# The order of large and small experts in a routed layer, small experts two chunks behind

## The chip, the cores and the metric

The kernel runs on one core of one Trainium2 chip. The metric is the device time of one execution in microseconds (us); each kernel is run several times and the median counts. All operands and results are float32; weights arrive from HBM in units of [128 x 2048] float32, 1 MB (1.0486 million bytes) each. Matrix products of the large experts are made of three products of rounded parts (float32r), those of the small experts of plain float32 ones.

## The reference, cut to what matters

Two decoder layers on 256 tokens of width 1024. Layer 0: differential attention beside a state-space model, then a dense SwiGLU. Layer 1: two kinds of attention, then eight routed SwiGLU experts of which each token uses two. The change touches the experts alone:

```python
def swiglu(h, w_gate, w_up, w_down):
    return (jax.nn.silu(h @ w_gate) * (h @ w_up)) @ w_down

def moe_swiglu(h, router, w_gate, w_up, w_down):
    ...
    logits = (t @ router).astype(jnp.float32)
    top_val, top_idx = lax.top_k(logits, TOP_K)
    top_w = jax.nn.softmax(top_val, axis=-1)
    gates = jnp.sum(jax.nn.one_hot(top_idx, N_EXPERTS, dtype=jnp.float32) * top_w[..., None], axis=1)
    for e in range(N_EXPERTS):
        out = out + gates[:, e:e + 1].astype(t.dtype) * swiglu(t, w_gate[e], w_up[e], w_down[e])
```

D_MODEL is 1024, D_FF 2816, N_EXPERTS 8, TOP_K 2.

## The kernel before, in words

The experts are put in order of their number of tokens at run time. The four with the most are called large (up to 128 tokens, kept in a tile of 128), the four with the fewest small (up to 64, kept in a tile of 64). If an expert has more than 128 tokens, a loop behind an `If` takes the rest; it does not run here. D_FF is cut in 11 chunks of 256. A chunk of an expert has three units of weights: two halves of the gate and up weights (`gu` unit 0 and 1, each 512 of the 1024 input rows) and one unit of the down weights (`dn`). Four large and four small experts make 88 chunks and 264 units.

A **large** chunk: each unit is split into a rounded part `wh` (ScalarE, `ACTIVATE wh`) and the rest `wl` (VectorE, `TENSOR_TENSOR wl`) by `split`, and each half of the gate and up product (`ff_gu`, 12 matmuls, L517 to L519, stationary `fh`, `fl`) and the down product (`ff_dn`, 12 matmuls, stationary `tw`) use them. Between them stand Silu and the multiplication (`ff_act`) and two transpositions on TensorE with their copies (`ff_tr`). A **small** chunk uses the weights as they arrive, in products on half of the array's columns (128*64, two at a time): `sm_gu` (8 matmuls of 256 columns a half unit pair, shown as 16 by the profile), `sm_act`, one transposition in `sm_tr`, `sm_dn` (4 matmuls of 512 columns, shown as 8). The products of an expert's chunks add up in two PSUM tiles; after its last chunk they are split (`y_split`) and scattered to the tokens (`scatter`, 8 matmuls). The tokens of an expert are gathered ahead by one-hot matmuls (`gather_all`, two or four of them a group).

`Stream` (L693) reads the units in the order of use. It has nine places that a unit can land in (five `raw`, and `xres`, `xg`, `more`, `fl`; a tenth until unit 14), and four pairs of tiles for `wh` and `wl` (`HL` = 4). A large unit's place comes free when it is split, a small unit's when TensorE has used it; SP issues the next unit's load into the place that came free first, and waits for it in order. `st.ahead(n)` splits the next large unit if fewer than n are split and unused.

Up to the first expert the order on each engine is written by a recording scheduler (`Recorder`); in the experts' stage the recorder is off (`rec.on = False`) and each engine does its instructions in the order in which the Python code writes them. That order is what the change edits. Before: `items` holds the chunks, large ones alone for the first four (`LAG` = 4), then large and small in turn, then four small ones. In the step of item i stand: first half of its gate and up product, the transpositions of item i-1 and its copies, a split ahead, the second half, Silu, the down product of item i-1. A small item's halves therefore have the transpositions of a large chunk between them, and a large item's halves that of a small chunk. The gathers and the scatter stand behind the down product.

Of the kernel before, what the change touches and what calls it, by code (L numbers as in the profile page):

```python
# [19 lines left out]
P = 128  # L20
EPS = 1e-6
NEG = -1e30
FC = 11
# [26 lines left out]
HL = 4  # L50
# [2 lines left out]
XG = 14  # L53
BIG = 4
HALFP = 64
LAG = 4
PAIRED = 0.65
WARM = 10
FIRST = 9
# [335 lines left out]
def kernel(ctx: ExitStack, tc: tile.TileContext, a, out: bass.AP):  # L395
# [32 lines left out]
    def pa():  # L428
        return rec.tile(psp, [P, 512], F32, "ps", 8, name="ps")
# [337 lines left out]
    def ff_gu(st, xs, gu, u, ahead=True):  # L767
        wh, wl = st.next(ahead)
        for b in range(len(xs)):
            for kk in range(4):  # L770
                k = 4 * u + kk
                mm3(gu[b], xs[b][0][:, k, :], xs[b][1][:, k, :], wh[:, kk * 512:(kk + 1) * 512],
                    wl[:, kk * 512:(kk + 1) * 512], k == 0, k == 7)

    def ff_act(gu, scales=None, act=None):
        hs = []
        for b in range(len(gu)):
            si = tw(256)
            hh = tw(256)
            if scales:  # L780
                tact(si, gu[b][:, 0:256], AF.Silu, scale=scales[b])
                V.scalar_tensor_tensor(hh, gu[b][:, 256:512], scales[b], si, op0=OP.mult, op1=OP.mult)
            else:
                (act or tact)(si, gu[b][:, 0:256], AF.Silu)
                V.tensor_tensor(hh, gu[b][:, 256:512], si, OP.mult)
            hs.append(hh)
        return hs

    def ff_tr(hs):
        n = 2 * len(hs) * P  # L790
        tp = pa()
        transposes([h[:, i * P:(i + 1) * P] for i in range(2) for h in hs], tp)
        th, tl = tw(n, dt=F32R), tw(n, dt=F32R)
        S.activation(th, tp[:, :n], AF.Copy)
        V.tensor_tensor(tl, tp[:, :n], th.bitcast(F32), OP.subtract)
        return th, tl

    def ff_dn(st, t, yps, first, last, ahead=True):
        wh, wl = st.next(ahead)
        nb = len(yps)  # L800
        order = [(b, i, hf) for b in range(nb) for i in range(2) for hf in range(2)]
        for b, i, hf in sorted(order, key=lambda o: o[2]) if last else order:
            rec.late = HALF if last and hf else 0
            sl = slice((i * nb + b) * P, (i * nb + b + 1) * P)
            ws = slice(i * 1024 + hf * 512, i * 1024 + (hf + 1) * 512)
            mm3(yps[b][hf], t[0][:, sl], t[1][:, sl], wh[:, ws], wl[:, ws], first and i == 0, last and i == 1)
# [63 lines left out]
    for g in range(2):  # L870
        ps = [pa() for i in range(2)]
        for u in range(2):
            wh, wl = split(raw0[u]) if g == 0 else unit(a["w0"][2 + u])
            for kk in range(4):
                k = 4 * u + kk
# [8 lines left out]
        for c in range(4):  # L884
            j = 4 * g + c
# [93 lines left out]
    for b in range(2):  # L979
        y = tw()  # L980
# [529 lines left out]
    def y_split(yps):  # L1510
        rec.late = 0
        y = [(tw(dt=F32R), tw(dt=F32R)) for i in range(2)]
        for i in range(2):
            rec.late = HALF if i else 0
            S.activation(y[i][0], yps[i], AF.Copy)
            V.tensor_tensor(y[i][1], yps[i], y[i][0].bitcast(F32), OP.subtract)
        return y

    def scatter(t, y, g, acc, store=False):
        for i in range(2):  # L1520
            rec.late = HALF if i else 0
            cs = slice(i * 512, (i + 1) * 512)
            for b in range(2):
                sp = pa()
                T.matmul(sp, t[:, b * P:(b + 1) * P], y[i][0], start=True, stop=False)
                T.matmul(sp, t[:, b * P:(b + 1) * P], y[i][1], start=False, stop=True)
                V.scalar_tensor_tensor(acc[:, b, cs], sp, g(b), acc[:, b, cs], op0=OP.mult, op1=OP.add)
                if store:
                    dma(ov[:, b, cs], acc[:, b, cs])
        rec.late = 0  # L1530
# [5 lines left out]
    def large_split(src):  # L1536
        x = large_tile()
        S.activation(x[0], src, AF.Copy)
        V.tensor_tensor(x[1], src, x[0].bitcast(F32), OP.subtract)
        return x  # L1540


    def sm_gu(xs, gu, u):
        w = st.next(False)
        for kk in range(4):
            k = 4 * u + kk
            wv = w[:, kk * 512:(kk + 1) * 512].rearrange("p (g f) -> p g f", g=2)
            for i in range(2):
                mmx(gu[i * HALFP:(i + 1) * HALFP, 0:256].rearrange("p (g f) -> p g f", g=2), xs[:, k],
                    wv[:, :, i * P:(i + 1) * P], k == 0, k == 7)  # L1550
        st.done()

    def sm_act(gu):
        si, hh = tw(P), tw(P)
        tact(si, gu[:, 0:P], AF.Silu)
        V.tensor_tensor(hh, gu[:, P:256], si, OP.mult)
        return hh

    def sm_tr(hh):
        tp = pa()  # L1560
        transposes([hh], tp)
        t = tw(P)
        S.activation(t, tp[:, 0:P], AF.Copy)
        return t
# [14 lines left out]
        return lambda: gtile([P, 2048], F32, n, 2) if n == "xres" else mo([P, 2048], n)  # L1579


    items = []
    for g in range(BIG * FC + LAG):
        if g < BIG * FC:
            items.append((False, *divmod(g, FC)))
        if g >= LAG:
            items.append((True, *divmod(g - LAG, FC)))
    regs = {}

    def source(r, j):  # L1590

        if r == 0:
            return a["moe"][j]

        def at_run():
            if r not in regs:
                regs[r] = nc.values_load(ids[0:1, r:r + 1], engines=[mybir.EngineType.SP], min_val=0, max_val=7)
            return a["moe"][bass.ds(regs[r] * (3 * FC) + j, 1)].rearrange("u p c -> p (u c)")
        return at_run

    srcs, whole = [], []
    for i in range(len(items) + 1):
        for it, js in ((items[i] if i < len(items) else None, (0, 1)), (items[i - 1] if i else None, (2,))):
            for j in js if it else ():
                srcs.append(source(it[1] + (BIG if it[0] else 0), 3 * it[2] + j))
                whole.append(it[0])
    st = Stream(srcs, ([(place("xres"), 999), (place("xg0"), XG)],
                       [(place("xg1"), 999), (place("more"), 999), (place("fl"), 999)]), whole)
    xb = large_tile()
# [6 lines left out]
    xs = top([P, BIG, 8, HALFP], "xs")  # L1616
    oh_s = one_hots(BIG, BIG, HALFP)
    ov = out.rearrange("(b p) d -> p b d", p=P)
    ys, ohs, ohts, hs, pend = {}, {}, {}, {}, None
    N = len(items)  # L1620
    for i in range(N + 1):
        it = items[i] if i < N else None
        was = items[i - 1] if i else None
        alone = not (it and was and it[0] != was[0])
        if it:
            sm, p, c = it
            gu = pa()
            xsp = xs[:, p] if sm else [xb]
            sm_gu(xsp, gu, 0) if sm else ff_gu(st, xsp, [gu], 0, False)
        if was:  # L1630
            t = sm_tr(hs[was]) if was[0] else ff_tr(hs[was])
        st.ahead(HL if alone or it[0] else HL - 1)
        if it:
            sm_gu(xsp, gu, 1) if sm else ff_gu(st, xsp, [gu], 1, False)
            hs[it] = sm_act(gu) if sm else ff_act([gu])
            if not sm and c == FC - 1 and p < BIG - 1:
                xb = large_split(xl[:, p % 2])
        if alone or it[0]:
            st.ahead(HL)
        if was:  # L1640
            wsm, wp, wc = was
            if wc == 0:
                ys[wsm] = [pa(), pa()]
            (sm_dn if wsm else lambda t, y, *f: ff_dn(st, t, [y], *f, False))(t, ys[wsm], wc == 0, wc == FC - 1)
            if alone:
                st.ahead(HL)
        if pend:
            scatter(*pend)
            pend = None
        if was and was[2] == FC - 1:  # L1650
            r = was[1] + (BIG if was[0] else 0)
            pend = (ohts[was[0]], y_split(ys[was[0]]), lambda b, r=r: gateo[:, b, r:r + 1], x3, i == N)
        if not it:
            continue
        if c == 0:
            ohs[sm] = both_halves(BIG + p) if sm else one_hots(p, 1)[:, :, 0]
        if c == 1:
            ohts[sm] = oht_of(ohs[sm][:, 0], ohs[sm][:, 1])
        if sm:
            continue  # L1660
        if p == 0 and c < LAG:
            for k in range(2 * c, 2 * c + 2):
                gather_all(k, oh_s, xs)
        if p == 0 and LAG + 2 <= c < LAG + 6:
            if c == LAG + 2:
                xl, oh_l = mo([P, 2, 8, P], "xg0"), one_hots(1, 2)
            for k in range(2 * (c - LAG - 2), 2 * (c - LAG - 1)):
                gather_all(k, oh_l, xl)
        if p == 1 and 2 <= c < 6:
            if c == 2:  # L1670
                oh_l = one_hots(3, 1)
            for k in range(2 * c - 4, 2 * c - 2):
                gather_all(k, oh_l, xl[:, 0:1])
    scatter(*pend)
    man.close()


# [177 lines left out]
```

## Time and profile before

| what | value |
|---|---|
| time, median of 3 runs | 1151.35 us (1151.13 to 1151.51) |
| the profiled execution's own time | 1150.8 us |
| its span | 1148.9 us, mean granted clock 0.994 |
| TensorE (PE) busy | 1124.3 us, 98% |
| VectorE (DVE) busy | 714.2 us, 62% |
| ScalarE (ACT) busy | 587.3 us, 51% |
| HBM read, written | 345.95 MB, 1.05 MB |
| experts' stage, from the first large product to the last down product | 468 to 1139 us |

A busy time of TensorE is a union of overlapping matmuls whose ends are modelled; how long a piece of its work takes is read from the start of one piece to the start of the next. Times of rows count from the start of the span. In the rows of a timeline, `x16` is a run of 16 instructions of one kind, and `[0.62 <-DVE tw L333]` is idle time ahead of it and what ended it. L333 is a helper's line, which stands for many operations; the tiles tell them apart: `ps<-cp,tw` is a transposition, `ps<-tw,xnh` and `ps<-tw,xnl` a gather, `ps<-tw` a scatter, 128*64 a small expert's product.

### The profile page before, as it was taken

To read this page: it belongs to the slowest core of one execution; us is meant where nothing else is said; L and a number is where in the kernel's file an instruction comes from. 1 tells how busy PE (TensorE), PEld (TensorE's weight loads), DVE (VectorE), ACT (ScalarE), POOL (GpSimd) and SP (SyncE) were. 2 spreads that over 40 slices of the span, in tenths; PEclk is the share of its full clock that TensorE was granted. 3 is DMA by queue.
4 is the path that set the end of the run, shared out by engine and by line. 5 is a ranking of instruction groups with operands and counts; after the bars stand their busy time and mean duration, and the time that the engine had idled before them with its cause. 6 is when DMAs were issued, how large, how long until landed. Compare 5 with 4: busy or idle time off the path is not lost.

```text
span 1148.9 us, 16368 instructions
## 1 busy us (share of the span) xinstructions
PE 1124.3 (98%) x6100; PEld 825.4 (72%) x6100; DVE 714.2 (62%) x1172; ACT 587.3 (51%) x979; POOL 29.6 (3%) x59
## 2 busy tenths in 40 slices
PE   8999999999999999999999999999999999999997
PEld 7887888888787877876666666666666666666663
DVE  6999954545388877784456456556556556565531
ACT  6858644444378666573545444444444444444421
POOL 1050000000300000000000000000000000000000
PEclk9999999999999999899999999999999999999999
DMA  9651555546344514389999999999999999999994
GB/s 353 224 198 37 195 208 189 189 179 219 112 167 154 216 63 188 117 325 373 374 404 419 399 400 392 393 424 422 421 421 422 422 423 420 422 421 418 421 421 157
DMA packets 52214, 348.14 MB, mean 303 GB/s; under 512 B 5920, under 2 KB 6048, under 8 KB 11680
## 3 DMA queue, kind: packets, MB, share of 16 engines
q1 hardware_dynamic: 52128, 347.02, 76.1%
q8 instruction: 50, 0.82, 0.3%
q14 instruction: 36, 0.29, 0.1%
HBM read 345.95 MB, written 1.05 MB: 302 GB/s over the span
## 4 chain that ended last, share of the span: by engine, by line
PE 84%; DMA 7%; DVE 5%; ACT 3%; issue 1%; SPq 0%; DVEq 0%; ACTq 0%
PE ps L333 21%; PE ps L517 18%; PE ps L519 18%; PE ps L518 18%; PE ps L328 10%; DMA xres<-in_moe_dram 7%; DVE wl L333 2%; ACT wh L333 2%; DVE wl L328 1%; ACT tw L328 1%; DVE xres L333 0%; DVE tw L328 0%; DMA raw<-in_w_dram 0%; DVE tw L333 0%; DVE more L328 0%
## 5 line engine op out<-in xcount | busy, mean ns | idle before, releaser
L333 DVE TENSOR_TENSOR wl<-raw,wh 128x2048 fp32r<-128x2048 f32 x89 | 204.2, 2294 | 149.5 <-ACT wh L333 148.0
L517 PE MATMUL ps<-wh,fh 128*128 128x512 f32 (+2 forms) x720 | 290.9, 404 | 0.0
L518 PE MATMUL ps<-wl,fh 128*128 128x512 f32 (+2 forms) x720 | 280.6, 390 | 0.0
L333 ACT ACTIVATE tw<-ps 128x128 f32<-128x128 f32 (+2 forms) x202 | 72.7, 362 | 312.1 <-PE ps L333 275.6
L333 ACT ACTIVATE wh<-raw 128x2048 fp32r<-128x2048 f32 x89 | 170.0, 1910 | 62.3 <-PE ps L519 57.7
L517 PEld LDWEIGHTS ps<-wh,fh 128*128 128x128 f32 x720 | 136.4, 189 | 28.1
L518 PEld LDWEIGHTS ps<-wl,fh 128*128 128x128 f32 x720 | 136.4, 189 | 24.1
L333 DVE TENSOR_TENSOR tw<-ps,tw 128x256 f32<-128x256 f32 (+3 forms) x158 | 66.7, 427 | 135.6 <-ACT tw L333 135.5
L519 PE MATMUL ps<-wh,fl 128*128 128x512 f32 (+2 forms) x368 | 142.1, 386 | 0.0
L519 PE MATMUL ps<-wh,fh 128*128 128x512 f32 x352 | 139.0, 395 | 0.0
L333 DVE TENSOR_TENSOR wl<-xres,wh 128x2048 fp32r<-128x2048 f32 x39 | 89.3, 2289 | 53.5 <-ACT wh L333 53.5
L333 PE MATMUL ps<-raw,xs 128*64 128x256 f32 x960 | 116.3, 384 | 0.0
L517 PE MATMUL ps<-wh,tw 128*128 128x512 f32 (+1 forms) x276 | 113.9, 413 | 0.7 <-ACT tw L328 0.7
L519 PE MATMUL ps<-wh,tw 128*128 128x512 f32 (+1 forms) x276 | 109.0, 395 | 0.0
L518 PE MATMUL ps<-wl,tw 128*128 128x512 f32 (+1 forms) x276 | 108.8, 394 | 0.0
L333 ACT ACTIVATE wh<-xres 128x2048 fp32r<-128x2048 f32 x39 | 74.8, 1917 | 63.4 <-DMA xres<-in_moe_dram 58.6
L328 DVE TENSOR_TENSOR wl<-raw,wh 128x512 fp32r<-128x512 f32 (+1 forms) x149 | 98.3, 683 | 2.7 <-ACT wh L328 2.7
L333 PEld LDWEIGHTS ps<-raw,xs 128*64 128x64 f32 x960 | 64.8, 137 | 41.3 <-issue 14.5
L328 ACT ACTIVATE wh<-raw 128x512 fp32r<-128x512 f32 (+1 forms) x131 | 74.8, 626 | 20.1 <-PE ps L519 8.6
L519 PEld LDWEIGHTS ps<-wh,fl 128*128 128x128 f32 x368 | 69.1, 188 | 14.3 <-DVE fl L328 0.2
L519 PEld LDWEIGHTS ps<-wh,fh 128*128 128x128 f32 x352 | 66.7, 189 | 14.5
L517 PEld LDWEIGHTS ps<-wh,tw 128*128 128x128 f32 x276 | 52.0, 188 | 26.4 <-issue 15.4
(283 smaller groups left out, 1324.9 us busy)
## 6 DMA issues: line engine op xcount, KB each, us to landing
raw<-in_moe_dram SPq DMA_DIRECT2D x142, 1024.0 KB, 9.6
xres<-in_moe_dram SPq DMA_DIRECT2D x41, 1024.0 KB, 10.5
raw<-in_ffn_dram SPq DMA_DIRECT2D x30, 1024.0 KB, 4.8
xg<-in_moe_dram SPq DMA_DIRECT2D x27, 1024.0 KB, 9.8
more<-in_moe_dram SPq DMA_DIRECT2D x26, 1024.0 KB, 10.8
fl<-in_moe_dram SPq DMA_DIRECT2D x25, 1024.0 KB, 9.7
raw<-in_w_dram SPq DMA_DIRECT2D x23, 1024.0 KB, 5.0
raw<-in_ffn_dram SPq DMA_DIRECT2D x12, 256.0 KB, 3.7
```

Of the source, the lines that this page charges most:

```text
L328: return (self.name, self.cost(fn, args, kw), lambda: real(*args, **kw))
L333: return getattr(self.eng, fn)(*args, **kw)
L517: nc.tensor.matmul(ps, xh, wh, start=start, stop=False)
L518: nc.tensor.matmul(ps, xh, wl, start=False, stop=False)
L519: nc.tensor.matmul(ps, xl, wh, start=False, stop=stop)
```

## The change

`LAG` goes from 4 to 2. The list of items becomes a list of steps (`tr` transpositions, `gu0` and `gu1` the halves, `dn` down product, `late` scatter, `rest` gathers and one-hots, `more` a split ahead), written once for each chunk of the large experts. In the mixed stretch it is: transpositions of the last large chunk, first half of the next, the scatter if there is one, the small chunk's transposition, large down product, second half, gathers, and then the three small units in one block: down product, first half, second half. A split ahead (now always to four) stands behind each transposition and behind the large down product. The eight gathers of the small experts come four a chunk in the first two large chunks instead of two a chunk in the first four.

```diff
-LAG = 4
+LAG = 2
...
-    items = []
-    for g in range(BIG * FC + LAG):
-        if g < BIG * FC:
-            items.append((False, *divmod(g, FC)))
-        if g >= LAG:
-            items.append((True, *divmod(g - LAG, FC)))
+    steps = []
+    for g in range(BIG * FC + LAG + 1):
+        l, l0, s, s0 = chunk(False, g), chunk(False, g - 1), chunk(True, g - LAG), chunk(True, g - LAG - 1)
+        if l and s0:
+            o = [("tr", l0), ("gu0", l), ("late", None), ("tr", s0), ("dn", l0), ("gu1", l), ("rest", l),
+                 ("dn", s0), ("gu0", s), ("gu1", s)]
+        elif l0:
+            o = [("gu0", l), ("tr", l0), ("gu0", s if not l else None), ("tr", s0), ("gu1", l), ("more", l), ("dn", l0),
+                 ("late" if l else "", None), ("rest", l), ("dn", s0), ("gu0", s if l else None), ("gu1", s)]
+        else:
+            o = [("gu0", l or s), ("tr", s0), ("gu1", l or s), ("more", l), ("dn", s0), ("late", None), ("rest", l)]
+        steps += [(k, it) for k, it in o if it or k == "late"]
...
-        st.ahead(HL if alone or it[0] else HL - 1)
...
+        elif k == "tr":
+            ts[sm] = sm_tr(hs[sm]) if sm else ff_tr(hs[sm])
+            st.ahead(HL)
+        elif k == "dn":
...
+                ff_dn(st, ts[sm], [ys[sm]], c == 0, c == FC - 1, False)
                 st.ahead(HL)
...
-            for k in range(2 * c, 2 * c + 2):
-                gather_all(k, oh_s, xs)
...
+                for j in range(8 // LAG * c, 8 // LAG * (c + 1)):
+                    gather_all(j, oh_s, xs)
```

On TensorE, in the mixed stretch, the small block and what follows it. `raw`, `more` and `xres` are places of small units, `cp` is the identity for a transposition. Before:

```order
L519 MATMUL ps<-wh,fh 128x512
L333 MATMUL ps<-raw,tw 64x512 x4
L333 MATMUL ps<-more,xs 64x256 x8
L333 MATMUL ps<-cp,tw 128x128 x2
L333 MATMUL ps<-raw,xs 64x256 x8
L517 MATMUL ps<-wh,tw 128x512
```

And the changed kernel at a like place:

```order
L519 MATMUL ps<-wh,fh 128x512
L333 MATMUL ps<-raw,tw 64x512 x4
L333 MATMUL ps<-raw,xs 64x256 x8
L333 MATMUL ps<-xres,xs 64x256 x8
L333 MATMUL ps<-cp,tw 128x128 x2
L517 MATMUL ps<-wh,fh 128x512
```

The large chunk's two transpositions moved from between the small halves to behind them, and behind them comes the large first half (stationary `fh`) where the large down product (stationary `tw`) came.

On ScalarE, one pair of a large and a small chunk. `wh` is a split, `tw` of 128x256 the large chunk's Silu or the copy behind its transpositions, `tw` of 128x128 the same of the small chunk. Before:

```order
L333 ACTIVATE wh<-raw 128x2048
L333 ACTIVATE tw<-ps 128x256 x2
L333 ACTIVATE wh<-fl 128x2048
L333 ACTIVATE tw<-ps 128x128
L333 ACTIVATE wh<-xres 128x2048
L333 ACTIVATE tw<-ps 128x128
```

And the changed kernel:

```order
L333 ACTIVATE tw<-ps 128x256
L333 ACTIVATE wh<-raw 128x2048
L333 ACTIVATE tw<-ps 128x128
L333 ACTIVATE wh<-more 128x2048
L333 ACTIVATE wh<-fl 128x2048
L333 ACTIVATE tw<-ps 128x256
L333 ACTIVATE tw<-ps 128x128
```

The three splits of a pair, which stood apart with one or two other instructions between them, stand closer: two of them follow each other, with the large chunk's Silu (128x256) right behind.

## Rows read from the trace of the kernel before

**Rows 1.** Two stretches: busy of PE, PEld, DVE, ACT, POOL; PEclk; DMA share; GB/s.
```profile
505.00:767.00 262.00, 260.88 (x1434) 175.53 (x1433) 144.25 (x129) 123.84 (x142) 0.00 (x0) 1.00 0.98 394
767.00:1110.00 343.00, 342.36 (x1861) 228.78 (x1860) 198.16 (x176) 157.44 (x169) 0.00 (x0) 1.00 1.01 421
```
**Rows 2.** Timeline of TensorE over one pair: start, us, instruction, run.
```profile
745.35 0.39 PE L519 MATMUL ps<-wh,fh 128*128 128x512 f32 x1
745.67 1.94 PE L333 MATMUL ps<-raw,tw 128*64 128x512 f32 x8
747.44 1.90 PE L333 MATMUL ps<-xg,xs 128*64 128x256 f32 x16
749.27 0.44 PE L333 MATMUL ps<-cp,tw 128*128 128x128 f32 x2
749.63 1.95 PE L333 MATMUL ps<-raw,xs 128*64 128x256 f32 x16
751.51 0.50 PE L517 MATMUL ps<-wh,tw 128*128 128x512 f32 x1
...
754.42 0.39 PE L517 MATMUL ps<-wh,fh 128*128 128x512 f32 x1
...
757.16 0.27 PE L333 MATMUL ps<-cp,tw 128*128 128x128 f32 x1
757.18 0.48 PE L517 MATMUL ps<-wh,fh 128*128 128x512 f32 x1
...
760.11 1.94 PE L333 MATMUL ps<-more,tw 128*64 128x512 f32 x8
```
**Rows 3.** Waits from 520 to 1110 us: who for whom, total us, times, longest.
```profile
ACT wh L333 <- DMA xres<-in_moe_dram: 58.6, 23, 4.3
...
PE ps L333 <- DVE tw L333: 1.8, 3, 0.6
```
**Rows 4.** The chain of waits, 937 to 953 us: start, us, what.
```profile
937.76 10.51 DMA xres<-in_moe_dram
...
948.34 1.93 ACT wh L333
...
952.61 11.61 DMA xres<-in_moe_dram
```
**Rows 5.** Timeline of TensorE where small chunks run alone.
```profile
1126.84 1.95 PE L333 MATMUL ps<-more,xs 128*64 128x256 f32 x16
1128.61 1.89 PE L333 MATMUL ps<-raw,tw 128*64 128x512 f32 x8
```
**Rows 6.** Timeline of TensorE where large chunks run alone.
```profile
479.75 0.38 PE L333 MATMUL ps<-cp,tw 128*128 128x128 f32 x2
479.88 0.48 PE L517 MATMUL ps<-wh,fh 128*128 128x512 f32 x1
...
482.71 0.40 PE L517 MATMUL ps<-wh,tw 128*128 128x512 f32 x1
```
**Rows 7.** The chain of waits at two pairs with a gather.
```profile
574.17 7.14 PE ps L333 x50
589.90 7.13 PE ps L333 x50
```
**Rows 8.** Timeline of TensorE at a gather with a wait, and at a scatter.
```profile
544.37 0.63 PE L333 MATMUL ps<-tw,xnh 128*128 128x256 f32 x2 [0.62 <-DVE tw L333]
...
790.86 2.11 PE L333 MATMUL ps<-tw 128*128 128x512 f32 x8
792.90 1.95 PE L333 MATMUL ps<-raw,xs 128*64 128x256 f32 x16
```
**Rows 9.** DMA from 505 us to the end: queue total; issues, KB, median us to landing.
```profile
q1 hardware_dynamic: 36853, 255.78, 96.9%
...
xg<-in_moe_dram SPq DMA_DIRECT2D x4, 256.0 KB, 5.3
```
**Rows 10.** Timeline of SP at the last loads: the last unit's four quarters.
```profile
1124.26 2.16 SPq L443 DMA_DIRECT2D xg<-in_moe_dram  x4
```

More of the change, by code (lines that the diff above doesn't have):

```diff
@@ L1579, in place, with chunk @@
         return lambda: gtile([P, 2048], F32, n, 2) if n == "xres" else mo([P, 2048], n)
-    items = []
-    for g in range(BIG * FC + LAG):
-        if g < BIG * FC:
-            items.append((False, *divmod(g, FC)))
-        if g >= LAG:
-            items.append((True, *divmod(g - LAG, FC)))
+    def chunk(sm, g):
+        return (sm, *divmod(g, FC)) if 0 <= g < BIG * FC else None
+    steps = []
[10 more added lines that the diff above has]
+        steps += [(k, it) for k, it in o if it or k == "late"]
     regs = {}
@@ L1599, in source @@
         return at_run
[L1601 to L1606, printed above, removed]
+    unit_of = {"gu0": 0, "gu1": 1, "dn": 2}
+    used = [(k, it) for k, it in steps if k in unit_of]
+    srcs = [source(it[1] + (BIG if it[0] else 0), 3 * it[2] + unit_of[k]) for k, it in used]
+    whole = [it[0] for k, it in used]
     st = Stream(srcs, ([(place("xres"), 999), (place("xg0"), XG)],
@@ L1618 @@
     ov = out.rearrange("(b p) d -> p b d", p=P)
[L1619 to L1631, printed above, removed]
-        st.ahead(HL if alone or it[0] else HL - 1)
[L1633 to L1638, printed above, removed]
-            st.ahead(HL)
[L1640 to L1645, printed above, removed]
-                st.ahead(HL)
[L1647 to L1661, printed above, removed]
-            for k in range(2 * c, 2 * c + 2):
-                gather_all(k, oh_s, xs)
[L1664 to L1673, printed above, removed]
@@ L1674 @@
-    scatter(*pend)
+    gu, hs, ts, ys, ohs, ohts, pend = {}, {}, {}, {}, {}, {}, []
+    for n, (k, it) in enumerate(steps):
+        if k == "late":
+            while pend:
+                scatter(*pend.pop(0))
+            continue
+        sm, p, c = it
+        if k == "more":
+            st.ahead(HL)
+        elif k in ("gu0", "gu1"):
+            if k == "gu0":
+                gu[sm] = pa()
+            if sm:
+                sm_gu(xs[:, p], gu[sm], unit_of[k])
+            else:
+                ff_gu(st, [xb], [gu[sm]], unit_of[k], False)
+            if k == "gu1":
+                hs[sm] = sm_act(gu[sm]) if sm else ff_act([gu[sm]])
+                if not sm and c == FC - 1 and p < BIG - 1:
+                    xb = large_split(xl[:, p % 2])
+                if c == 0:
+                    ohs[sm] = n, both_halves(BIG + p) if sm else one_hots(p, 1)[:, :, 0]
+        elif k == "tr":
+            ts[sm] = sm_tr(hs[sm]) if sm else ff_tr(hs[sm])
+            st.ahead(HL)
+        elif k == "dn":
+            if c == 0:
+                ys[sm] = [pa(), pa()]
+            if sm:
+                sm_dn(ts[sm], ys[sm], c == 0, c == FC - 1)
+            else:
+                ff_dn(st, ts[sm], [ys[sm]], c == 0, c == FC - 1, False)
+                st.ahead(HL)
+            if c == FC - 1:
+                r = p + (BIG if sm else 0)
+                pend.append((ohts[sm], y_split(ys[sm]), lambda b, r=r: gateo[:, b, r:r + 1], x3, n == len(steps) - 2))
+        else:
+            for e in list(ohs):
+                if n >= ohs[e][0] + 5:
+                    o = ohs.pop(e)[1]
+                    ohts[e] = oht_of(o[:, 0], o[:, 1])
+            if p == 0 and c < LAG:
+                for j in range(8 // LAG * c, 8 // LAG * (c + 1)):
+                    gather_all(j, oh_s, xs)
+            if p == 0 and LAG + 2 <= c < LAG + 6:
+                if c == LAG + 2:
+                    xl, oh_l = mo([P, 2, 8, P], "xg0"), one_hots(1, 2)
+                for j in range(2 * (c - LAG - 2), 2 * (c - LAG - 1)):
+                    gather_all(j, oh_l, xl)
+            if p == 1 and 2 <= c < 6:
+                if c == 2:
+                    oh_l = one_hots(3, 1)
+                for j in range(2 * c - 4, 2 * c - 2):
+                    gather_all(j, oh_l, xl[:, 0:1])
```

## The prediction

> **What bounds the kernel now.** I read the stretches of the expert stage first, to see which engine is full. TensorE is busy throughout, at a granted clock of 1.00, and the DMA engines have a share of 0.98 at 394 GB/s from 505 to 767 us and of 1.01 at 421 GB/s from 767 to 1110 us [rows 1]. Both look full, and a busy share does not tell who waits for whom. So I went to TensorE's instructions in order of time. One pair (the three units of a large chunk and the three of a small one) runs from 745.67 to 760.11 us, 14.44 us, without an idle time worth naming [rows 2]; from 520 to 1110 us the largest wait of TensorE for another engine sums to 1.8 us [rows 3]. TensorE sets the pace. But the weights are close behind: one pair needs six units of 1.0486 MB, which at 421 GB/s take 14.94 us, more than the pair's 14.44. That the memory stream has caught up shows in the chain of waits: a landing in `xres`, on its way from 937.76 us, releases ScalarE's split at 948.34, which with VectorE's releases the next landing at 952.61 [rows 4], a loop of 14.85 us; and ScalarE waited 58.6 us in 23 places for such landings, 4.3 us at most [rows 3]. TensorE hardly felt these, because the weights are split well ahead of their use. So there are two limits half a microsecond a pair apart, and the change moves only one of them.
>
> **The change part by part.** No product is added or removed: 36 large and 20 small products and three transpositions a pair stay, and the same 264 units are read. What moves is the order.
>
> *The small block.* Today a pair is, by the starts of its pieces [rows 2]: small down product 1.77, small first half 1.83, the large chunk's two transpositions 0.36, small second half 1.88, large down product 2.91, large first half with the small transposition 2.76, large second half 2.93; sum 14.44. After the change the two small halves follow each other and the transpositions stand behind them, ahead of the large first half. Priced from rows: small down product 1.77; first small half, going straight on in small products, 1.77 (1126.84 to 1128.61) [rows 5]; second small half, followed by a transposition, 1.83; large first half behind transpositions 2.83 (479.88 to 482.71) [rows 6] and 0.02 for the small transposition (757.16 to 757.18) [rows 2]; large down product behind a transposition 2.91, as today behind a change of the kind of product; large second half 2.93 less the slowed start of 0.09 (2.83 of [rows 6] less the 2.74 that the first half takes without its transposition) = 2.84. The two transpositions cost 0.13 between large products (479.75 to 479.88) [rows 6] and 0.36 between small ones; behind them now comes a large product, so I take 0.17, near the first. Sum 1.77 + 1.77 + 1.83 + 0.17 + 2.83 + 0.02 + 2.91 + 2.84 = 14.14, 0.30 less (0.34 with 0.13, 0.11 with 0.36). There are 40 pairs with a transposition inside the small block, so 12.0 us (4.4 to 13.6).
>
> The row shows the price of going from large to small products: 745.35 to 745.67 is 0.32 us where 0.23 is the large products' own spacing [rows 2]. The Trainium skill, "TensorEngine Tiling (Array Packing)", Key Properties, says that changing the tiling mode drains the engine. By that alone two changes fewer a pair at 0.09 us would give 7 us over 40 pairs; the trace has the rest in the slowed start behind each change, so the sum of rows stands.
>
> *Gathers, scatters and one-hot transpositions.* Today the gathers of the later large experts (eight groups of eight matmuls) and three of the scatters stand inside the small block; they go to where large products are on at least one side. A pair with a gather takes 15.73 us (574.17 to 589.90) [rows 7], 1.29 more than one without; a scatter there takes 2.04 (790.86 to 792.90) [rows 8], and its eight products at the large spacing of 0.23 would take 1.84. I take 0.2 for each of the eleven places and 0.25 for three one-hot transpositions, 3 us (bounds 0, and 14 times the 0.36 of [rows 2], 5).
>
> *Two chunks behind instead of four.* Two large and two small chunks that ran alone become pairs. Alone or paired the products are the same, and the price of a pair, 14.14, is that of its parts, so I put 0 (bounds: two pairs at 0.34 either way). The eight gathers of the small experts are the same eight, four a chunk instead of two; VectorE and ScalarE have room beside a large chunk. For the stream it matters a little: a large chunk alone asks for three units in some 8.5 us, slower than it can be fed.
>
> TensorE alone therefore needs 12 + 3 = 15 us less (4 to 19).
>
> *The weights.* Three splits a pair remain, but they now stand together in the large block: one ahead of the large first half, one behind the small transposition, one behind the large down product; none is asked for in the small block. Behind a split that waits for its landing, ScalarE's queue holds the small chunk's copy and the large chunk's Silu, whose product the next large transposition needs. The copy has the large down product and second half as cover (5.8 us), the Silu the small block (5.4 us); a wait of the size seen today, 4.3 us, is hidden there, and beyond that it reaches TensorE one for one. SP's queue still takes the units in the order of use.
>
> What the stream can give: from 505 us on the queue of loads and stores moved 255.78 MB [rows 9], of which 1.05 are stored, so 254.7 MB of weights; at 421 GB/s that is 605 us, to 1110 us. The last quarter of the last unit was issued at 1126.42 (1124.26 + 2.16) [rows 10] and lands 5.3 us later [rows 9], at 1131.7. So 21.7 us are there for an idle-free stream, 16.8 of them (262 us x (421 - 394) / 421) before 767 us [rows 1]. What TensorE would ask: with a small chunk two behind, 41 pairs x 14.14 + gathers 8 x 1.1 (1.29 less 0.2) + six scatters x 1.85 + 1 = 600 us for 41 x 14.94 = 612.5 us of stream. The difference of 12.5 us must come out of the lead of the landing over the use. That lead I estimate at 10 us: a landing takes 5.3 us when the queue is short [rows 9] and 10.5 to 11.6 us when it is full [rows 4], so some 5.5 us go into the queue, and a wait of 4.3 us on ScalarE is hidden. It falls short by 2.5 us; and the stage starts with three units split ahead instead of four, one place later freed, which I put at 1.5 us by half of one split's use (2.83). So 4 us of the 15 come back as waits (0 to 10 as the lead is 13 or 5).
>
> **Sum.** 15 - 4 = 11 us less, against the profiled execution: its span of 1148.9 us becomes 1137.9. That execution took 1150.8 us in all, 0.55 under the median of 1151.35; I take 11 off the median: 1140.4 us. From both sides: 19 off with no wait, 4 off with the small price and the waits of this estimate left in its own slack: 1132 to 1147.
>
> What the stream can carry is first the row's 421 GB/s over 343 us. The Trainium skill, "HBM Reference", Specifications (TRN2), gives about 425 GB/s for one core that streams alone, bounded by its 16 DMA engines; the trace agrees to 1%, so nothing the order of TensorE does can lift it. By 425 the stream would end 6 us earlier, and the forecast would lean towards the first rival.
>
> **The rivals.**
>
> *TensorE takes all of it.* The lead holds to the end and the waits do not come. For it: TensorE waits nowhere today though ScalarE does [rows 3]. Against it: 14.94 us of stream a pair against 14.14. Then 15 to 19 us off: 1134 us.
>
> *The stream gets no sooner.* The splits, bunched in the large block, free their places in bursts, the DMA engines still run dry between the bursts as they do before 767 us [rows 1], and the 16.8 us stay lost. TensorE then runs faster into a stream that is no faster, and what it gains it waits. For it: the loop through `xres` [rows 4] is a loop of landing and split, and no part of it gets shorter. Against it: in the mixed stage places are asked for every 14.1 instead of 14.4 us. No change: 1151 us.
>
> *Slower: ScalarE's queue holds up the transposition in each pair.* The place is the split behind the large down product: it waits for TensorE and for its landing, with the Silu queued behind it. If each pair costs TensorE 0.62 us, which is what a wait ahead of a gather costs at 544.37 us today [rows 8], 41 pairs make 25 us against 15 saved, 10 us slower: 1161 us. It decides from 15 / 41 = 0.37 us a pair upwards. For it: none of the splits falls into the small block any more, so the queue is denser where it counts. Against it: the covers of 5.4 and 5.8 us.
>
> **How the numbers follow.** I give 0.60 to the forecast, 0.20 to TensorE taking all, 0.12 to the stream that gets no sooner, 0.08 to the slower case. The range 1132 to 1147 holds the first two and some of the third. A change under 0.2% (2.3 us) cannot be told from none in a measurement of this kernel. Faster by more: nearly all of the first two and a third of the third, 0.83; within: 0.09; slower: 0.08.
>
> **What would show it.** Right: a pair near 14.1 us in the first experts, 14.9 in the later ones; DMA at 421 GB/s from about 520 us on; more waits of ScalarE for landings than 58.6 us; the last unit landing near 1117 us. The small block from its down product to the transpositions takes 5.4 us. Wrong: a pair that stays at 14.4 (the price of the transposition was not in the array changes); idle time of TensorE ahead of the large transposition in every pair (the third rival); GB/s under 400 up to 767 us (the second).

## The result and the profile after

The changed kernel takes 1164.97 us (median of 6 runs, 1161.52 to 1166.83), the kernel before 1151.24 us beside it: a ratio of 1.0121, 95% interval 1.0102 to 1.0139. It is slower by some 14 us, where 11 us less was forecast. The profiled execution took 1166.83 us, its span 1165.1 us.

| | before | after |
|---|---|---|
| span, mean granted clock | 1148.9 us, 0.994 | 1165.1 us, 0.984 |
| TensorE busy | 1124.3 us (98%) | 1118.3 us (96%) |
| VectorE, ScalarE busy | 714.2, 587.3 us | 717.0, 593.6 us |

TensorE has less to do and yet ends later. The two stretches of [rows 1], after the change:

```profile
505.00:767.00 262.00, 253.89 (x1414) 176.25 (x1413) 143.77 (x126) 123.48 (x138) 0.00 (x0) 0.98 0.97 395
767.00:1110.00 343.00, 328.84 (x1792) 226.66 (x1791) 193.97 (x171) 157.34 (x164) 0.00 (x0) 0.98 0.99 407
```

The DMA engines moved 395 and 407 GB/s where 421 was expected throughout; TensorE stands 8 and 14 us idle in them, and its granted clock is below 1.00. An undisturbed pair, though, is what the prediction made of it; TensorE's timeline, as in [rows 2]:

```profile
588.01 1.94 PE L333 MATMUL ps<-raw,tw 128*64 128x512 f32 x8
589.78 1.90 PE L333 MATMUL ps<-raw,xs 128*64 128x256 f32 x16
591.51 1.90 PE L333 MATMUL ps<-xg,xs 128*64 128x256 f32 x16
593.34 0.44 PE L333 MATMUL ps<-cp,tw 128*128 128x128 f32 x2
593.53 0.48 PE L517 MATMUL ps<-wh,fh 128*128 128x512 f32 x1
...
602.11 1.08 PE L333 MATMUL ps<-raw,tw 128*64 128x512 f32 x4
```

From 588.01 to 602.11 are 14.10 us (14.14 predicted), the small block up to the transpositions 5.33 (5.4), the transpositions 0.19 (0.17). So the products cost what was said, and the loss lies in waits. Who waited for whom from 520 to 1110 us, as [rows 3]:

```profile
ACT wh L333 <- DMA raw<-in_moe_dram: 73.7, 23, 4.9
...
PE ps L333 <- DVE tw L333: 14.3, 11, 2.4
ACT wh L333 <- DMA fl<-in_moe_dram: 12.5, 19, 1.8
ACT wh L333 <- DMA more<-in_moe_dram: 11.9, 22, 1.8
...
PE ps L517 <- DVE xres L333: 4.6, 3, 1.9
...
PE ps L517 <- ACT tw L333: 2.5, 3, 1.1
...
PE ps L519 <- DVE fh L333: 0.7, 3, 0.2
```

TensorE waits 22.1 us (14.3, 4.6, 2.5 and 0.7) instead of 1.8, and ScalarE 98 us for landings, where it waited 60 (58.6 of them for `xres`). Three things in the trace could have started this, and I made each a theory.

*T1, the late stream.* With `LAG` 2 the ninth unit in the order of use is a small expert's, whose address is known only at run time; `Stream.load` holds such a load back while the recorder is on. 8 units instead of 14 are loaded ahead of the stage, and the loads go on only at 467.26 us; before, six more were issued from 436 to 463 us. The prediction did not see it.

*T2, the changes of expert.* TensorE's waits stand mostly at 620 to 645, 790 to 825 and 960 to 992 us, where VectorE's additions of the scatter and the copies of a finished expert are queued behind a split that waits for its landing.

*T3, swapped places.* It came up only after the first four experiments. SP, which issues the loads, in a stretch without any change of expert:

```profile
716.61 0.33 SPq L443 DMA_DIRECT2D more<-in_moe_dram  x1
719.24 0.33 SPq L443 DMA_DIRECT2D fl<-in_moe_dram  x1
720.43 2.06 SPq L443 DMA_DIRECT2D raw<-in_moe_dram  x2
723.88 0.33 SPq L443 DMA_DIRECT2D xg<-in_moe_dram  x1
734.52 0.33 SPq L443 DMA_DIRECT2D raw<-in_moe_dram  x1
735.11 0.33 SPq L443 DMA_DIRECT2D more<-in_moe_dram  x1
735.71 0.33 SPq L443 DMA_DIRECT2D fl<-in_moe_dram  x1
```

For 10 us nothing is issued, then three loads at once. Yet VectorE had finished the split that in the code frees the place for the load at 734.52 long before:

```profile
726.46 2.29 DVE L333 TENSOR_TENSOR wl<-raw,wh 128x2048 fp32r<-128x2048 f32 x1 [1.38 <-ACT wh L333]
```

It ended at 728.75; the load came 5.8 us later, right behind the small down product (732.54 to 734.48). The five `raw` places are one ring of tiles, and which of the five a new tile gets is settled when the program is built. The instructions as built show it (a listing of the program, not a view of the profile). The six loads of that pair in the changed kernel (`PE` in a wait is TensorE, `DVE` VectorE; the `DMAHW` ones, waits for earlier transfers, are left out here):

```
raw<-in_moe   waits PE      (behind it in the queue: all that follow)
more<-in_moe  waits DVE
fl<-in_moe    waits DVE
raw<-in_moe   no wait
raw<-in_moe   waits PE
xres<-in_moe  waits PE
```

The load made behind the split of unit 100 was given the place of unit 97, a small down unit that TensorE had yet to use; the place of unit 100, free since 728.75, went to the load made behind unit 97's use. SP issued in order, so the load into `more`, whose place was free since 731.51 us (the end of its split on VectorE), and the one into `fl` stood behind it until 735.11 and 735.71. The same swap stands 25 times in the changed kernel's stage, in runs that begin at units 46, 106, 160 and 226. At each beginning the DMA engines run dry: over the 9 us around the four they moved 174, 215, 235 and 228 GB/s, the second from 731 to 740 us:

```profile
731.00:740.00 9.00, 9.00 (x59) 5.57 (x58) 3.86 (x5) 2.37 (x5) 0.00 (x0) 1.00 0.57 215
```

### The profile page after: what moved, and what is told of

It reads as the page before. It is cut to its first block, busy times and chain, and to the rows that moved or that the text cites. A ratio compares the mean times of both kernels' runs of the same rounds, so it can differ in the third digit from the quotient of the medians.

```text
span 1165.1 us, 16298 instructions
## 1 busy us (share of the span) xinstructions
PE 1118.3 (96%) x6100; PEld 835.5 (72%) x6100; DVE 717.0 (62%) x1172; ACT 593.6 (51%) x979; POOL 29.5 (3%) x59
## 4 chain that ended last, share of the span: by engine, by line
PE 75%; DMA 14%; DVE 4%; ACT 4%; issue 2%; SPq 0%; ACTq 0%; DVEq 0%
PE ps L333 17%; PE ps L517 16%; PE ps L519 16%; PE ps L518 16%; PE ps L328 10%; DMA fl<-in_moe_dram 8%; DMA more<-in_moe_dram 3%; ACT wh L333 3%; DMA raw<-in_moe_dram 2%; DVE wl L333 1%; DVE wl L328 1%; ACT tw L328 1%; DVE tw L328 0%; DMA raw<-in_w_dram 0%; DVE xres L333 0%
## 5 line engine op out<-in xcount | busy, mean ns | idle before, releaser
L333 DVE TENSOR_TENSOR wl<-raw,wh 128x2048 fp32r<-128x2048 f32 x71 | 162.9, 2295 | 193.9 <-ACT wh L333 193.9
L333 ACT ACTIVATE tw<-ps 128x256 fp32r<-128x256 f32 (+3 forms) x202 | 72.3, 361 | 269.3 <-PE ps L333 239.0
L333 ACT ACTIVATE wh<-raw 128x2048 fp32r<-128x2048 f32 x71 | 135.8, 1912 | 132.3 <-DMA raw<-in_moe_dram 78.1
L333 DVE TENSOR_TENSOR tw<-ps,tw 128x128 f32<-128x128 f32 (+3 forms) x158 | 66.3, 428 | 154.1 <-ACT tw L333 153.8
L517 PEld LDWEIGHTS ps<-wh,fh 128*128 128x128 f32 x720 | 136.9, 190 | 25.2
L333 DVE TENSOR_TENSOR wl<-more,wh 128x2048 fp32r<-128x2048 f32 x42 | 96.2, 2291 | 23.3 <-ACT wh L333 23.2
L333 DVE TENSOR_TENSOR wl<-fl,wh 128x2048 fp32r<-128x2048 f32 x41 | 94.0, 2292 | 14.8 <-ACT wh L333 14.4
L333 ACT ACTIVATE wh<-fl 128x2048 fp32r<-128x2048 f32 x41 | 78.6, 1916 | 37.3 <-PE ps L519 22.7
L333 ACT ACTIVATE wh<-more 128x2048 fp32r<-128x2048 f32 x42 | 80.4, 1915 | 19.3 <-DMA more<-in_moe_dram 19.3
L333 PE MATMUL ps<-raw,tw 128*64 128x512 f32 x336 | 84.0, 622 | 1.5 <-ACT tw L333 1.5
## 6 DMA issues: line engine op xcount, KB each, us to landing
xg<-in_moe_dram SPq DMA_DIRECT2D x22, 1024.0 KB, 13.3
```

The lines of the kernel that those rows point to most:

```text
L333: return getattr(self.eng, fn)(*args, **kw)
L517: nc.tensor.matmul(ps, xh, wh, start=start, stop=False)
```

## The experiments

All ratios are to the kernel before on the same chip, with 95% intervals.

**LAG alone undone.**

```diff
-LAG = 2
+LAG = 4
```

> The changed kernel with LAG back at 4 (large experts four chunks ahead, gathers two a chunk in four chunks); the new order of steps stays. Two theories. T1, the late stream: with LAG 2 the ninth unit of the stream already is a small expert's, whose address is known only at run time, so only 8 units instead of 14 can be loaded ahead, and the six units' 15 us of transfer are missing later; with LAG 4 the first 14 units have a known address again. T1 expects 1138 to 1147 us (the 15 us that the order saves TensorE come through). T2, the order: splits that wait for a landing hold the one-hots, the second part of the next expert's tokens and the scatter's additions back on VectorE and ScalarE at the changes of expert, whatever the stream's start; it expects 1156 to 1166 us, with the waits of TensorE at 620 to 645, 790 to 825 and 960 to 992 us still there.

1158.27 us, ratio 1.0082 (1.0062 to 1.0103): 6.7 us less than the change by the medians, 4.5 by the ratios, whose intervals just touch. That is far from the 15 of T1, and inside T2's range.

**LAG alone done**, in the old order of items.

```diff
-LAG = 4
+LAG = 2
...
-            for k in range(2 * c, 2 * c + 2):
+            for k in range(8 // LAG * c, 8 // LAG * (c + 1)):
```

> The kernel before with LAG 2 alone (its old order of items, small experts two chunks behind, gathers four a chunk). T1 (late stream) expects the loss without the gain: 1158 to 1168 us, with the load of unit 8 behind the loading of the first run-time address. T2 (order) expects the time of before within 3 us: 1149 to 1154 us.

1151.60 us, ratio 1.0012 (1.0002 to 1.0022). With the stream starting as late as in the changed kernel the old order loses about 1 us. That speaks against T1, and for the prediction's 0 for `LAG`.

**The first small units' address known.**

```diff
-        if r == 0:
-            return a["moe"][j]
+        if r == 0 or (r == BIG and j < 3):
+            return a["moe"][(3 * FC if r else 0) + j]
```

> The changed kernel with its order and LAG 2, but the three units of the first chunk of the first small expert are read from a fixed address (another expert's first chunk), so that 14 units can again be loaded before the run-time addresses are known. It computes that one chunk with the wrong weights. T1 expects all or most of the 15 us back: 1145 to 1152 us, units 8 to 13 issued before 465 us. T2 expects 1161 to 1166 us: the early loads only move the first wait.

1164.92 us, ratio 1.0129 (1.0110 to 1.0148). The loads came early again (six issued from 436 to 463 us), and the time is that of the changed kernel. T1 is out as the cause of the loss. My reading: an early start fills the places sooner, and they are all that the stream can run ahead by.

**One split moved into the small block.**

```diff
-                 ("dn", s0), ("gu0", s), ("gu1", s)]
+                 ("dn", s0), ("more", l), ("gu0", s), ("gu1", s)]
```

> The changed kernel with one of the three splits of a pair moved: behind the small down product instead of behind the large transposition, so that one of the splits falls into the small block as before. T1 expects 1162 to 1167 us, since the stream starts as late as in the changed kernel. T2 expects a good part of the loss back, 1148 to 1157 us: places come free evenly and Silu no longer has two splits in front of it.

1169.49 us, ratio 1.0152 (1.0134 to 1.0169): slower still, against T2's half of the expectation. TensorE's waits from 520 to 1110 us:

```profile
PE ps L333 <- DVE tw L333: 23.6, 21, 2.9
```

The split now stands ahead of the small Silu, whose product the small transposition needs 3 us later. The waits went from the changes of expert to half the pairs. Spreading the splits was no cure. It does not clear their bunching either, because it brings waits of its own, and 24 loads behind splits have swapped places in this program too. The next experiment, which leaves the splits where they are, decides that.

**Fixed places.** Each of the five raw places becomes one tile that is loaded again and again; a load then waits for the split or the product that freed this place.

```diff
-            self.free, self.used = [(raw_tile, len(srcs))] * RAW + list(more[0]), []
+            def fixed():
+                t = []
+                return lambda: t[0] if t else t.append(raw_tile()) or t[0]
+
+            raws = [(fixed(), len(srcs)) for k in range(RAW)] if whole else [(raw_tile, len(srcs))] * RAW
+            self.free, self.used = raws + list(more[0]), []
```

> The changed kernel with one thing changed: each of the five raw places of the stream is one tile that is loaded again and again, so that a load waits for the split or the product that freed its place in the order of the code. In the changed kernel the program, as built, gives the large half unit that is loaded behind a split the place of a small expert's down unit instead, which is used some 6 us later in the pair, and all loads behind it in SP's queue wait too. Theory T3, the swapped places: that is where the DMA engines run dry (units 46, 89, 106, 160, 226); it expects these stalls gone, DMA above 0.99 from 520 us, and 1140 to 1155 us. The rival T2 (the order at the changes of expert holds VectorE and ScalarE behind waiting splits) expects 1160 to 1166 us, the waits at 620 to 645, 790 to 825 and 960 to 992 us unchanged.

1147.01 us, ratio 0.9965 (0.9953 to 0.9978): 18.0 us less than the change, by this alone, and faster than before. T3's range holds, T2's is missed by 13 us. The splits are bunched as they were, so the bunching by itself was not the cause of these 18 us. SP at the like place of the program:

```profile
717.56 2.06 SPq L443 DMA_DIRECT2D raw<-in_moe_dram  x2
721.01 0.33 SPq L443 DMA_DIRECT2D xg<-in_moe_dram  x1
725.92 0.33 SPq L443 DMA_DIRECT2D raw<-in_moe_dram  x1
728.68 0.33 SPq L443 DMA_DIRECT2D more<-in_moe_dram  x1
731.31 0.33 SPq L443 DMA_DIRECT2D fl<-in_moe_dram  x1
```

What SP's queue waited for from 520 to 1110 us, first in the changed kernel, then with fixed places:

```profile
SPq L443 <- PE ps L333: 291.1, 75, 11.2
SPq L443 <- DVE wl L333: 115.8, 40, 4.5
```
```profile
SPq L443 <- DVE wl L333: 268.1, 81, 4.5
SPq L443 <- PE ps L333: 105.2, 82, 5.7
```

The longest wait for a product falls from 11.2 to 5.7 us, and the loads wait for splits again. The stretches of [rows 1]:

```profile
505.00:767.00 262.00, 257.07 (x1431) 179.10 (x1430) 146.49 (x127) 126.55 (x141) 0.00 (x0) 0.98 0.99 409
767.00:1110.00 343.00, 337.05 (x1867) 232.82 (x1866) 201.20 (x176) 162.38 (x169) 0.00 (x0) 1.00 1.01 421
```

From the landings of units 15 to 260, what each came later than 2.5 us behind the one before it sums to 38.5 us in the changed kernel and 20.1 us here, a difference as large as that of the times. The four loads at the beginnings of the runs of swaps (46, 106, 160, 226) make 13.8 us of the 38.5; here none of them is late by more than 0.6. (The stall at unit 89, which the expectation names too, is no swap: it stays here, and goes with the one-hots below.)

**Fixed places in the kernel before**, the same edit.

> The kernel before with the same fixed raw places. In it too the built program swaps places, but between units that are used close together. T3 expects a small gain at most, 1145 to 1151 us, since TensorE bounds this kernel; T2 expects the time of before within 2 us.

1149.98 us, ratio 0.9996 (0.9987 to 1.0005): nothing. In the old order 36 loads behind splits have swapped places too, without harm to the time: the SP of the kernel before waits for a product at most 5.0 us. So a swap alone costs nothing here; the new order is exposed to it. My reading, not tried by itself: with the three small units in one block behind three large ones, the place of a small down unit comes free some 6 us after that of a split.

**Fixed places with LAG 4**, the edits of the first and the fifth experiment together.

> The changed kernel with LAG 4 and fixed raw places. T3 expects what the prediction said of the new order, 1136 to 1146 us, under the kernel before. T2 expects the 1158 us of LAG 4 alone within 4 us.

1148.64 us, ratio 0.9983 (0.9974 to 0.9992). Fixing the places gains 9.6 us at this LAG too. It does not reach what T3 expected: something else is still lost.

**Fixed places and early one-hots.** After fixing, TensorE still stood 2.4 us ahead of the first gathers. In the changed kernel:

```profile
523.16 0.39 PE L519 MATMUL ps<-wh,fh 128*128 128x512 f32 x1
525.89 0.63 PE L333 MATMUL ps<-tw,xnh 128*128 128x256 f32 x2 [2.35 <-DVE tw L333]
```

The gathers now follow the second large half directly, and the one-hots they need stand on VectorE behind that half's Silu product. Before, the small down product lay between, and the wait was 0.62 us [rows 8].

```diff
             if k == "gu0":
                 gu[sm] = pa()
+                if not sm and (p, c) == (0, LAG + 2):
+                    xl, oh_l = mo([P, 2, 8, P], "xg0"), one_hots(1, 2)
+                if not sm and (p, c) == (1, 2):
+                    oh_l = one_hots(3, 1)
```

(and the same calls taken out of the gathers' step)

> The changed kernel with fixed raw places, and the one-hots of the large experts' gathers made three products earlier (ahead of the large first half), so that the first gather of a group doesn't wait for them behind Silu's product. TensorE waited 2.7 and 2.6 us there at 523 and 666 us. If those waits count, 4 to 7 us less than with fixed places alone; if the stream sets the end, within 2 us of it.

1143.02 us, ratio 0.9940 (0.9926 to 0.9953): 4.0 us less, the low end of what was expected if the waits count. Its stretches:

```profile
505.00:767.00 262.00, 260.43 (x1475) 183.15 (x1475) 153.22 (x130) 130.99 (x144) 0.00 (x0) 1.00 1.01 421
767.00:1110.00 343.00, 337.48 (x1859) 233.15 (x1857) 197.82 (x174) 160.93 (x169) 0.00 (x0) 0.99 1.01 420
```

Now the stream runs at 421 GB/s from the start, as the prediction had it, and the last unit lands at 1118.8 us, where the prediction put it near 1117. What TensorE still waits for, from 520 to 1110 us:

```profile
PE ps L517 <- DVE xres L333: 4.6, 3, 1.9
PE ps L517 <- ACT tw L333: 1.8, 3, 1.0
PE ps L333 <- DVE tw L333: 0.7, 1, 0.7
```

All of it stands at the three changes of a large expert. The pairs there take 18.25, 20.06 and 22.98 us, where a later pair with a scatter (826.36 to 842.53) and none of these waits takes 16.16. Pairs without either keep the short price, 14.09 to 14.10 us, to the end:

```profile
1050.78 1.94 PE L333 MATMUL ps<-raw,tw 128*64 128x512 f32 x8
...
1064.88 1.94 PE L333 MATMUL ps<-raw,tw 128*64 128x512 f32 x8
...
1078.97 1.94 PE L333 MATMUL ps<-raw,tw 128*64 128x512 f32 x8
```

**The scatter behind the large down product**, on top of that.

```diff
-            o = [("tr", l0), ("gu0", l), ("late", None), ("tr", s0), ("dn", l0), ("gu1", l), ("rest", l),
+            o = [("tr", l0), ("gu0", l), ("tr", s0), ("dn", l0), ("late", None), ("gu1", l), ("rest", l),
```

> Fixed places and early one-hots, and the scatter moved from ahead of the small transposition to behind the large down product. At each change of a large expert the first down product of the next one waits for two PSUM tiles that the scatter's additions free, and these stand behind a split on VectorE (waits of up to 1.9 us at 805 us, with a stretch at half the clock behind). If TensorE bounds the repaired kernel these three places are worth 3 to 8 us: 1135 to 1140 us. If the stream does, which runs at 421 GB/s from 520 us on in the kernel with early one-hots, the time stays within 2 us of 1143.

1156.90 us, ratio 1.0054 (1.0042 to 1.0067): 14 us slower, outside both expectations. I had overlooked that the down product that ends an expert hands its result to the next `late` step: the scatter now came in the same pair, right behind the copies of the result it needs.

```profile
623.79 0.39 PE L519 MATMUL ps<-wh,tw 128*128 128x512 f32 x1
627.99 0.79 PE L333 MATMUL ps<-tw 128*128 128x512 f32 x1 [3.81 <-ACT tw L333]
```

TensorE's waits from 520 to 1110 us rise from 7.1 to 18.8 us, 13.3 of them for these copies, and the time by 13.9: though the stream had been full, what TensorE waits reaches the end. The stream did not stay full, either: from 767 to 1110 us it moved 409 GB/s instead of 420. My reading is that both limits lie this close together.

**The known address, with places and one-hots mended.** The third edit again.

> Fixed places and early one-hots, with the first small chunk's three units read from a fixed address, so that 14 units are loaded ahead again (that chunk gets another expert's weights). T1, the late stream, gave nothing in the changed kernel. If the stream is the limit now that the places are fixed, the earlier start should be worth something here: 1133 to 1140 us. If TensorE is, 1141 to 1145 us.

1140.78 us, ratio 0.9917 (0.9905 to 0.9930). The 2.2 us under the kernel without it are within the spread of its 6 runs (1138.75 to 1145.44): at most a small part of T1. The median lies between the two expectations and decides for neither.

**LAG 4, with places and one-hots mended.**

> Fixed places and early one-hots with LAG 4: 14 units with a known address, but two more large chunks alone at the start and two more small ones alone at the end. As LAG 4 cost 1.6 us with fixed places, 1143 to 1146 us; by T1 (the late stream matters when the stream is the limit) 1136 to 1141 us.

1141.80 us, ratio 0.9925 (0.9912 to 0.9938), between the two expectations; the intervals of this and of LAG 2 overlap. The LAG matters little either way once the places are fixed.

**The split behind the scatter**, on top of LAG 4.

```diff
-            while pend:
-                scatter(*pend.pop(0))
+            if pend:
+                while pend:
+                    scatter(*pend.pop(0))
+                if n < len(steps) - 4:
+                    st.ahead(HL)
...
-            st.ahead(HL)
+            if sm or not pend:
+                st.ahead(HL)
```

> Fixed places, early one-hots and LAG 4; where a scatter waits, the split behind the large transposition is made behind the scatter instead of ahead of it, so that the scatter's additions stand ahead of that split on VectorE. The scatter stays where it is. If the additions behind a waiting split are what holds the next expert's first down product (up to 1.9 us at three changes of expert, with a stretch at half the clock behind), 3 to 6 us less than 1141.8. If the places freed 4.7 us later cost as much of the stream, no change within 2 us.

1140.58 us, ratio 0.9912 (0.9899 to 0.9926). The waits for `xres` are gone, others of 7.8 us in all stand in their place (7.7 with the edit undone), and ScalarE waits 108.3 us for landings instead of 39.7. The time is within 2 us of the kernel without the edit, as the second expectation has it. T2 is worth 1.2 us by this edit, less than the intervals tell apart; what the waits left at the changes of expert are worth by themselves stays open. By its median this is the fastest kernel here, 9.7 us under the one before beside it.

## Why the prediction was wrong, step by step

- *The price of a pair*: right, 14.10 us measured for 14.14, in the changed kernel and to the end of the mended one. So were the small block and the transpositions.
- *LAG at 0*: right in the old order (1 us) and with fixed places (1.6 us one way, with early one-hots 1.2 the other). Only in the changed kernel as it stands is it 4.5 to 6.7 us; there it also changes which loads swap places. That it shortens the loading ahead by six units was missed, and cost little or nothing.
- *"SP's queue still takes the units in the order of use", and so what the stream can give, 421 GB/s without idle time*: this is the step that failed. The order of use held; the place that each load waits for did not follow it. I took "the place that came free first" from the code's list and did not look at what each load waits for in the program as built. There, in the waits of SP's instructions, the swap was to be seen. 18.0 us by the fifth experiment.
- *Gathers, 0.2 us saved in each place*: wrong in sign for the first of each group. In this order nothing covered the one-hots between Silu's product and the first gather; 4.0 us by the experiment on them.
- *4 us given back as waits when the lead runs out*: not shown. In a few pairs of the changed kernel, within its third run of swaps, the stream does set the pace. The chain of waits runs through `fl` there as through `xres` in [rows 4], 14.87 us a turn (936.23 to 951.10), where 14.94 was worked out:

```profile
936.23 10.49 DMA fl<-in_moe_dram
...
946.83 1.93 ACT wh L333
...
951.10 10.48 DMA fl<-in_moe_dram
```

  With places and one-hots mended, where the forecast's stream is there, the later pairs don't go to the 14.9 us foretold: those without gather or scatter stay at 14.1, and ScalarE waits 31.5 us for landings, not more than 58.6. In place of the stream's waits stand those at the changes of expert. The three pairs there take 12.8 us more in all than three of 16.16; the sum had nothing for that.

- *The rivals*: the one called "the stream gets no sooner" named the outcome (DMA engines dry, 395 GB/s up to 767 us against 394 before) but gave it 0.12 and a floor of no change; behind 767 us the rate fell, from 421 to 407. Its mechanism, places freed in bursts by bunched splits, was not the cause: with fixed places the splits are as bunched and the stream runs at 409 and 421. The slower rival, a wait in each pair, did not come in the changed kernel; the experiment with the moved split shows what it looks like.

With the two faults mended and nothing else the kernel takes 1143.0 us against the 1140.4 forecast; the two missing terms were 22 us. That the rest comes within 2.6 us is in part luck: the 12.8 us at the changes of expert, which the sum lacked, stand where it had 4 us of the stream's, and by this count TensorE saved some 6 us more elsewhere than was put down. The stream ran at 421 GB/s where places were free. The Trainium skill's figure in "HBM Reference", Specifications (TRN2), about 425 GB/s for a core that streams alone, agrees with that again.

## What to carry to other kernels

When a change reorders who frees a buffer, read on the issuing queue what each load waits for in the built program; an in-order queue passes one late place on to every load behind it. Where buffers of one ring are freed by different engines, give each place its own tile (18.0 us here, nothing in the old order). And a producer moved next to its consumer has lost its cover, even if nothing else changes.

## What the runs showed that I had not expected

Short waits of TensorE can cost twice. Two stretches of the changed kernel, each behind waits:

```profile
526.00:530.00 4.00, 4.00 (x14) 2.17 (x16) 0.08 (x1) 0.95 (x2) 0.00 (x0) 0.57 1.02 426
...
819.00:827.00 8.00, 6.14 (x16) 4.76 (x16) 6.07 (x6) 3.17 (x2) 0.00 (x0) 0.57 1.01 419
```

Ahead of the first TensorE waited 2.35 us; in the 14 us ahead of and within the second 1.39, 1.00 and 1.86 us. The granted clock there is 0.57 on average, so for most of it the lower of the two levels (1.2 and 2.4 GHz):

```profile
821.54 0.63 PE L518 MATMUL ps<-wl,tw 128*128 128x512 f32 x1
821.97 0.63 PE L519 MATMUL ps<-wh,tw 128*128 128x512 f32 x1
```

The matmuls start 0.43 us apart instead of 0.23. In the kernel before, whose waits in this stage are 0.62 us at most [rows 3], the clock shows 1.00 in both stretches of [rows 1]. Not every wait is followed by such a stretch: behind one of 1.48 us at 795.93 in the changed kernel, and one of 1.71 us at 667.30 in the old order with `LAG` 2, the clock stays at 1.00. From 505 to 1135 us the stretches at the lower level sum to 23.8 us in the changed kernel, 13.6 with fixed places and 10.2 with early one-hots too, so part of what each of these two edits gave back is the clock; how much was not tried by itself.
